# Four early groups of the output projection in the mixer, with the attention's space handed to the FFN's weights

## The chip, the cores and the metric

The kernel runs on one core of a Trainium2 chip. The time is the device time of one execution in microseconds (us); lower is better. TensorE (PE) multiplies, PEld is its loading of weights, VectorE (DVE) and ScalarE (ACT) work elementwise, GpSimd (POOL) does masks and issues the weight DMAs of the staged parts, SyncE (SP) issues the other DMAs. TensorE writes into PSUM, which has 8 banks.

## The reference

Two layers over 528 tokens (16 learned meta tokens ahead of 512) of width 1024, each with a mixer and an FFN:

```python
def mixer_sublayer(h, ...):
    u = rms_norm(h, pre_g)
    z = einsum("bld,de->ble", u, w_in)
    q, k, v, f_logit, a_val, a_gate, sc_b, sc_c, sc_x = split(z)
    y_attn = forgetting_attention(q, k, v, log_sigmoid(f_logit + b_forget))   # 8 heads of 64
    a = a_val * sigmoid(a_gate)
    a = causal_depthwise_conv(a, a_dw_w) + a_dw_b                             # 31 taps, 256 channels
    y_conv = silu(layer_norm(a, a_ln_g, a_ln_b)) @ a_pw_w
    y_sc = sc_b * causal_depthwise_conv(sc_c * sc_x, sc_conv_w)               # 3 taps, 256 channels
    y = concat([y_attn, y_conv, y_sc])
    return h + rms_norm(head_rms_norm(y, head_g) @ w_out, post_g)

def ffn_sublayer(h, ...):
    z = causal_depthwise_conv(rms_norm(h, pre_g) @ w_up, conv_w)              # 3 taps, 2 x 2816 channels
    g, up = split(z, 2)
    return h + rms_norm((silu(g) * up) @ w_down, post_g)
```

All of it is in float32.

## The kernel before

Everything lies transposed: 128 channels on the partitions, tokens along a row, in two halves of 264 (`H`), `hf` 0 and 1. A float32 product is made of three passes over rounded parts, `hi*hi + lo*hi + hi*lo` (`mm3`, line 671), so each block of 128 output channels and each of its 8 blocks `k` of inputs costs three matmuls for a half. A weight block is brought by a DMA into `raw`, ACT casts it to `whi` (L625) and DVE makes the rest `wlo` (L629). `raw` has 3 buffers. `whi` and `wlo` have 3 buffers each in the pool of ring "rot" and 5 each (`WIDE`) in the wide pool, which is there only outside the mixers. `wide_ids` tells which blocks go into the wide pool.

The order of instructions on each engine is fixed when the kernel is built. In the mixers and around them a planner (`Flow`) sets it: generators ("threads") emit TensorE's work and yield what they wait for, other engines' operations are queued with priorities, and the planner goes through estimated times. On the chip each engine runs its list in that order.

The mixer first finishes the convolution's gates, then runs these threads together. `fill` makes the projections from `uhi`, `ulo`, with the convolution's tail and the norms as threads that it starts. `maxima` (L1402, L1426) finds each row's maximum of the attention logits with DVE's help (`mcol`). `exponentials` (L1448) makes the logits again and has ACT take the exponentials `p`. `weighing` (L1494) multiplies them with the values, for a pair of heads at a time. `att_norms` (L1560) and `plain_head_norm` (L1176) make the head norms: a product with the matrix `bd` gives the means of squares in a PSUM bank; ACT, DVE, DVE, ACT and DVE then make the normed parts `yhi` (L1163) and `ylo` (L1164). `y` 0 to 3 are attention's, 4 and 5 the convolution's (after a pointwise product with `pw`), 6 and 7 the gated convolution's (`sccx`, L1088).

PSUM banks are handed out by rings in the mixer: "mm" 0 and 1 for projections and all norms and products of the convolutions, "s1" 3 and 4 for maxima and attention's norms, "st" 5 and 6 for logits, "acc" 2 and 7 for the weighing.

`Early` starts part of the output projection `w_out` inside the mixer: the first pair of its 8 blocks (blocks 0 and 1), for each half of the tokens, as the `y` become ready. Half 0 takes banks 0 and 1 once `maxima` and `fill` are over, half 1 takes 5 and 6 once `exponentials` is over too. `finish` then has the rest: it copies the early results out (`evac`: L1693 to `yp`, L759 squares for the norm), makes the products of blocks 2 to 7 from one pair of banks at a time, and follows with the norm, the residual and the FFN's first products.

Attention's tiles (`q`, `k`, `p`, `vals`, sums) lie in a pool `ap` at the right side, which is closed at the mixer's end; the wide pool `wy` for the FFN then opens in that space.

## Time and profile before

| | |
|---|---|
| median of 3 runs | 1301.84 us (1299.65 to 1301.91) |
| profiled execution, its own time | 1300.12 us |
| its span, first to last instruction | 1298.4 us |
| mean granted clock | 0.995 |
| TensorE busy | 1271.5 us, 98% of the span |
| DVE, ACT, POOL busy | 894.8, 612.8, 110.2 us |

"Busy" is the time in which at least one instruction of the engine runs; matmuls overlap, so their count in a stretch says more than the busy time. A row of the waits names the instruction that waited and the one that released it. In a row of a timeline stand start and duration in us, engine, line, operation, output<-inputs, shape, count, and in brackets how long the engine was idle before and what ended that. A line number is that of the kernel before, unless the text says otherwise.

### The profile page before, as it was taken

What the parts mean: (1) busy time and instruction counts of PE and PEld (TensorE: products, weight loads), DVE (VectorE), ACT (ScalarE), POOL (GpSimd) and SP (SyncE); (2) the same over time, 40 slices, a digit from 0 to 9 for tenths busy, and PEclk for the clock granted to TensorE, in tenths of its full rate; (3) what the DMA queues carried; (4) which work ended last, traced back from release to release, by engine and by line L of the source; (5) the groups of instructions that cost most, each with busy time, mean ns of one, the idle gap of its engine ahead of it and who ended that gap; (6) DMA issues with size and microseconds to landing.
All of it is one profiled execution on the core that took longest, in us unless ns stands there. A gap on an engine that the chain in (4) does not pass through costs nothing. (4 is left out here: it accounts for less than half of the span.)

```text
span 1298.4 us, 24320 instructions
## 1 busy us (share of the span) xinstructions
PE 1271.5 (98%) x9922; PEld 1216.3 (94%) x9922; DVE 894.8 (69%) x1563; ACT 612.8 (47%) x1144; POOL 110.2 (8%) x270
## 2 busy tenths in 40 slices
PE   8999999999999999999999999989999999999997
PEld 7989978999999999999999898889999799989997
DVE  7888896688734775677568886756876256636664
ACT  7255568655433442444562445666543234314443
POOL 1311210100000000000203222100000000000000
PEclk9999999999999999999999999999999999999999
DMA  6133123515644556754542453414032222232321
GB/s 222 50 101 80 45 83 100 182 63 200 223 159 158 202 176 235 237 201 145 214 158 98 118 163 122 129 63 147 22 96 96 97 86 92 72 119 89 92 72 65
DMA packets 55440, 164.57 MB, mean 127 GB/s; under 512 B 6352, under 2 KB 16720, under 8 KB 55328
## 3 DMA queue, kind: packets, MB, share of 16 engines
q1 hardware_dynamic: 41200, 109.56, 25.5%
q0 software_dynamic: 14128, 53.45, 12.8%
q8 instruction: 78, 1.28, 0.4%
q14 instruction: 34, 0.28, 0.1%
HBM read 131.17 MB, written 27.46 MB: 122 GB/s over the span
## 5 line engine op out<-in xcount | busy, mean ns | idle before, releaser
L671 PE MATMUL psum<-uhi,whi 128*128 128x264 f32 (+1 forms) x1936 | 452.2, 287 | 1.0 <-ACT uhi L1865 0.9
L671 PE MATMUL psum<-ulo,whi 128*128 128x264 f32 (+1 forms) x1936 | 445.1, 284 | 0.5 <-DVE ulo L1867 0.4
L671 PE MATMUL psum<-uhi,wlo 128*128 128x264 f32 (+1 forms) x1936 | 444.7, 283 | 0.0
L671 PEld LDWEIGHTS psum<-uhi,whi 128*128 128x128 f32 x1936 | 322.5, 188 | 3.2 <-ACT uhi L1865 1.1
L671 PEld LDWEIGHTS psum<-ulo,whi 128*128 128x128 f32 x1936 | 322.1, 188 | 1.8 <-DVE ulo L902 0.6
L671 PEld LDWEIGHTS psum<-uhi,wlo 128*128 128x128 f32 x1936 | 322.3, 189 | 0.0
L671 PE MATMUL psum<-yhi,whi 128*128 128x264 f32 (+3 forms) x888 | 250.3, 305 | 6.7 <-ACT whi L625 2.2
L671 PE MATMUL psum<-yhi,wlo 128*128 128x264 f32 (+3 forms) x888 | 247.2, 300 | 0.9 <-DVE wlo L629 0.7
L671 PE MATMUL psum<-ylo,whi 128*128 128x264 f32 (+3 forms) x888 | 247.0, 300 | 0.6 <-DVE ylo L1164 0.5
L476 ACT CAST whi<-raw 128x1024 fp32r<-128x1024 f32 (+1 forms) x110 | 113.1, 1030 | 184.6 <-PE psum L671 146.1
L477 DVE TENSOR_TENSOR wlo<-raw,whi 128x1024 fp32r<-128x1024 f32 (+1 forms) x110 | 131.7, 1199 | 65.0 <-ACT whi L476 63.3
L671 PEld LDWEIGHTS psum<-yhi,whi 128*128 128x128 f32 x888 | 160.4, 190 | 14.6 <-ACT yhi L1163 2.6
L671 PEld LDWEIGHTS psum<-ylo,whi 128*128 128x128 f32 x888 | 160.6, 190 | 7.0 <-DVE ylo L1164 1.3
L671 PEld LDWEIGHTS psum<-yhi,wlo 128*128 128x128 f32 x888 | 160.8, 190 | 6.6 <-DVE wlo L629 1.3
L1968 DVE SCALAR_TENSOR_TENSOR c<-z,pv,c 128x528 f32<-128x528 f32 (+1 forms) x176 | 131.9, 756 | 2.7
L617 POOL DMA_DIRECT2D raw<-in_w_dram x60 | 32.1, 535 | 922.2 <-DVE wlo L477 703.9
L629 DVE TENSOR_TENSOR wlo<-raw,whi 128x1024 fp32r<-128x1024 f32 (+2 forms) x64 | 75.7, 1197 | 30.9 <-ACT whi L625 30.5
L987 DVE SCALAR_TENSOR_TENSOR cacc<-apad,pv,cacc 128x528 f32<-128x528 f32 x120 | 87.5, 763 | 0.9
L625 ACT CAST whi<-raw 128x1024 fp32r<-128x1024 f32 (+2 forms) x64 | 64.6, 1028 | 30.7 <-PE psum L671 16.0
L1978 ACT ACTIVATE c<-c 128x528 f32<-128x528 f32 (+1 forms) x44 | 28.1, 639 | 84.0 <-DVE c L1968 84.0
L1986 ACT CAST yhi<-c 128x528 fp32r<-128x528 f32 (+1 forms) x44 | 27.5, 625 | 84.4 <-DVE c L1982 84.2
L1966 ACT ACTIVATE c<-z,pv 128x528 f32<-128x528 f32 (+1 forms) x88 | 63.4, 727 | 0.1
(223 smaller groups left out, 1473.1 us busy)
## 6 DMA issues: line engine op xcount, KB each, us to landing
raw<-in_w_dram SPq DMA_DIRECT2D x116, 512.0 KB
raw<-in_w_dram POOLq DMA_DIRECT2D x44, 512.0 KB, 4.3
split_w<-whi SPq DMA_DIRECT2D x20, 512.0 KB
split_w<-wlo SPq DMA_DIRECT2D x20, 512.0 KB
whi<-split_w POOLq DMA_DIRECT2D x20, 512.0 KB, 4.7
wlo<-split_w POOLq DMA_DIRECT2D x20, 512.0 KB, 6.2
raw<-in_w_dram SPq DMA_DIRECT2D x20, 448.0 KB
raw<-in_w_dram POOLq DMA_DIRECT2D x12, 448.0 KB, 3.6
```

Source lines behind the costliest of these rows:

```text
L476: nc.scalar.copy(hi[:, :sz], raw[:, :sz])
L477: nc.vector.tensor_sub(lo[:, :sz], raw[:, :sz], hi[:, :sz].bitcast(F32))
L617: nc.gpsimd.dma_start(to, src)
L625: nc.scalar.copy(box["hi"][:, :sz], box["raw"][:, :sz])
L629: nc.vector.tensor_sub(lo[:, :sz], box["raw"][:, :sz], box["hi"][:, :sz].bitcast(F32))
L671: nc.tensor.matmul(d, lhsT=w[a][:, k, cols], rhs=rhs(b, k, hf), start=start and i == 0 and p == 0, stop=stop and i == n - 1 and p == 2)
L987: nc.vector.scalar_tensor_tensor(conv[j], in0=src, in1=conv[j], scalar=col("a_dw_w", CK * j + i), op0=ALU.mult, op1=ALU.add)
L1966: nc.scalar.activation(dst, src[:, 2:2 + 2 * fw], AF.Copy, scale=wtap(2, t))
L1968: nc.vector.scalar_tensor_tensor(dst, in0=src[:, i:i + 2 * fw], scalar=wtap(i, t), in1=dst, op0=ALU.mult, op1=ALU.add)
L1978: silu = nc.scalar.activation(cs[0], cs[0], AF.Silu)
L1986: nc.scalar.copy(ghi, cs[0])
```

## The change

- `Early` now works on four groups, named `(m0, hf)`: blocks 0 and 1 and also blocks 2 and 3, for both halves. `(0, 1)` begins when `exponentials` is over, `(0, 0)` when `maxima` and `fill` are. `(2, 0)` begins in banks 2 and 3 when all four attention threads are over, `(2, 1)` in banks 4 and 7 when the mixer is.
- When the attention threads are over, the pool `ap` is closed inside the mixer, the wide pool is opened in its place and the planner is given blocks 2 and 3, which `wide_ids` now puts there (with 6 and 7, instead of 5 to 7). The tile `pw` moves to the pool `mp`, since the convolution still needs it.
- PSUM: "s1" becomes banks 4 and 7, "acc" 2 and 3. The norms and products of the convolutions take a bank of "acc", or else of "mm"; `grab` can wait for the sooner of several rings.
- `finish` copies the four early groups out in a thread of its own and makes products for blocks 4 to 7. The rings of the FFN's start take over the banks of the early groups.

```diff
-            if m > KD - SPLIT[c[0]]:
+            if m > KD - SPLIT[c[0]] + (c[0] == "w_out") or c[0] == "w_out" and m in (2, 3):
                 out.add(i)
...
-    def grab(self, ring, slot=None):
+    def grab(self, ring, slot=None, *more):
         while True:
-            t = ring.slots[0].time
-            ...
-            yield [Head(ring)]
+            for r in (ring, *more):
+                t = r.slots[0].time
+                if t is not None and t <= self.pe:
+                    slot = slot or Slot()
+                    r.take(slot)
+                    return slot
+            yield [Soonest([Head(r) for r in (ring, *more)])]
...
-        ap = ms.enter_context(tc.tile_pool(name=f"ap{l}", bufs=1, side="right", reuse_waits="tile"))
-        banks = {"mm": Ring((0, 1)), "s1": Ring((3, 4)), "st": Ring((5, 6)), "acc": Ring((2, 7))}
+        aps = ExitStack()
+        ap = aps.enter_context(tc.tile_pool(name=f"ap{l}", bufs=1, side="right", reuse_waits="tile"))
+        banks = {"mm": Ring((0, 1)), "s1": Ring((4, 7)), "st": Ring((5, 6)), "acc": Ring((2, 3))}
...
-                ps, slot = yield from bank("mm")
+                ps, slot = yield from bank("acc","mm")
...
-        pw_place[0] = lambda: T(ap, [P, 1024], F32R, "pw")
+        pw_place[0] = lambda: T(mp, [P, 1024], F32R, "pw")
...
-            if over >= {"maxima", "fill"} and 0 not in early.t and name in ("maxima", "fill"):
+            if name == "exponentials":
+                early.begin(0, 1, PAIRS[1], *banks["st"].slots)
+            if over >= {"maxima", "fill"} and name in ("maxima", "fill"):
                 pair = list(banks["mm"].slots)
                 banks["mm"].slots = banks["s1"].slots
-                early.begin(0, PAIRS[0], *pair)
-            if over == {"maxima", "fill", "exponentials"}:
-                early.begin(1, PAIRS[1], *banks["st"].slots)
+                early.begin(0, 0, PAIRS[0], *pair)
+            if over >= attention and name in attention:
+                pair = list(banks["acc"].slots)
+                banks["acc"].slots = banks["s1"].slots
+                aps.close()
+                opened.append(wide_pool(f"wy{l}"))
+                plan_w(after_mixer[l] + 2)
+                early.begin(2, 0, 2, *pair)
...
-        flow.run(lambda: len(over) == 3 and flow.settled())
-        return y, y_at, early
+        flow.run(lambda: len(over) == 5 and flow.settled())
+        early.begin(2, 1, 4, *banks["s1"].slots)
+        return y, y_at, early, opened[0]
...
-        wxs = wide_pool(f"wy{l}", [early.slot[hf] for hf in range(2)])
+        taken = [[early.slot[2, hf], Slot()] for hf in range(2)]
+        for (one, also), i in zip(taken, (3, 7)):
+            also.buf = i
+            also.close(one)
+        p_rings([early.slot[0, hf] for hf in range(2)], *taken)
```

The order of instructions moves as follows at the places of which the prediction speaks. TensorE at the end of layer 0's mixer, from the last head norm's matmul on, before (`whi_249` and `whi_266` are blocks 0 and 1):

```order
L1176 MATMUL psum_1_67<-apad_290_2667,bd_11_93 128x264
L671 MATMUL psum_1_67<-yhi5_292_2678,whi_249_2239 128x264
L671 MATMUL psum_1_67<-ylo5_293_2679,whi_249_2239 128x264
L671 MATMUL psum_1_67<-yhi5_292_2678,wlo_253_2299 128x264
L671 MATMUL psum_1_67<-yhi5_292_2678,whi_266_2430 128x264
L671 MATMUL psum_1_67<-ylo5_293_2679,whi_266_2430 128x264
L671 MATMUL psum_1_67<-yhi5_292_2678,wlo_271_2467 128x264
L671 MATMUL psum_1_67<-yhi4_294_2690,whi_249_2239 128x264
```

and the same place after (`whi_286` and `whi_288` are blocks 2 and 3; lines are those of the changed kernel):

```order
L1181 MATMUL psum_1_67<-apad_290_2686,bd_11_93 128x264
L675 MATMUL psum_1_67<-yhi2_225_2041,whi_288_2661 128x264
L675 MATMUL psum_1_67<-ylo2_226_2042,whi_288_2661 128x264
L675 MATMUL psum_1_67<-yhi2_225_2041,wlo_294_2701 128x264
L675 MATMUL psum_1_67<-yhi3_270_2526,whi_286_2643 128x264
L675 MATMUL psum_1_67<-ylo3_271_2527,whi_286_2643 128x264
L675 MATMUL psum_1_67<-yhi3_270_2526,wlo_289_2672 128x264
L675 MATMUL psum_1_67<-yhi3_270_2526,whi_288_2661 128x264
```

Before, products on `y5` of the first half follow at once, and those on the second half, which wait for this norm, after 12 matmuls. Now products of the new groups with attention's `y` stand there, and 45 matmuls in all before the first that needs this norm. In layer 1 it is 54.

TensorE in layer 1, at the end of the last head's maxima (`mcol`) and the start of its logits (`q30`), before:

```order
L1402 MATMUL psum_1_67<-k30_764_7985,q30_772_7993 128x264
L1448 MATMUL psum_1_67<-q20_770_7991,k20_762_7983 16x16
L1448 MATMUL psum_1_67<-q21_771_7992,k21_763_7984 16x16
L1402 MATMUL psum_1_67<-k30_764_7985,q30_772_7993 128x264
L1426 MATMUL psum_1_67<-ident_r_6_76,mcol_907_9554 1x16
L1426 MATMUL psum_1_67<-ident_r_6_76,mcol_907_9554 1x128 x4
L1448 MATMUL psum_1_67<-q30_772_7993,k30_764_7985 128x16
L1448 MATMUL psum_1_67<-q31_773_7994,k31_765_7986 128x16
```

and after:

```order
L1431 MATMUL psum_1_67<-ident_r_6_76,mcol_906_9559 1x16
L1431 MATMUL psum_1_67<-ident_r_6_76,mcol_906_9559 1x128 x3
L1453 MATMUL psum_1_67<-q20_770_7991,k20_762_7983 16x16
L1453 MATMUL psum_1_67<-q21_771_7992,k21_763_7984 16x16
L675 MATMUL psum_1_67<-uhi_16_106,whi_885_9370 128x264
L675 MATMUL psum_1_67<-ulo_17_107,whi_885_9370 128x264
L675 MATMUL psum_1_67<-uhi_16_106,wlo_886_9371 128x264
L675 MATMUL psum_1_67<-uhi_16_106,whi_885_9370 128x264
L675 MATMUL psum_1_67<-ulo_17_107,whi_885_9370 128x264
L675 MATMUL psum_1_67<-uhi_16_106,wlo_886_9371 128x264
L675 MATMUL psum_1_67<-uhi_16_106,whi_885_9370 128x264
```

Nine matmuls of a projection (`uhi`, `ulo`) now stand between the maxima's rows, the last of which follows them, and six more behind that one. In layer 0's last round nine such matmuls come in as well.

ACT behind the last `y` of layer 0, before and after:

```order
L1163 CAST yhi4_294_2690<-cacc_279_2546 128x264
L1693 ACTIVATE yp_304_2782<-psum_1_67,pg0_3_70 128x264 x2
L759 ACTIVATE acc_313_2813<-psum_1_67 128x528
L1693 ACTIVATE yp_304_2782<-psum_1_67,pg0_3_70 128x264 x2
L759 ACTIVATE acc_314_2828<-psum_1_67 128x528
L625 CAST whi_315_2837<-raw_258_2319 128x1024
L625 CAST whi_316_2849<-raw_312_2797 128x1024
L625 CAST whi_318_2853<-raw_272_2473 128x1024
```

```order
L1168 CAST yhi4_297_2715<-cacc_277_2552 128x264
L1708 ACTIVATE yp_305_2832<-psum_1_67,pg0_3_70 128x264 x2
L763 ACTIVATE acc_314_2861<-psum_1_67 128x528
L1708 ACTIVATE yp_305_2832<-psum_1_67,pg0_3_70 128x264 x2
L763 ACTIVATE acc_317_2887<-psum_1_67 128x528
L1708 ACTIVATE yp_305_2832<-psum_1_67,pg0_3_70 128x264 x2
L763 ACTIVATE c_318_2905<-psum_1_67 128x528
L629 CAST whi_319_2914<-raw_313_2847 128x1024
L629 CAST whi_320_2926<-raw_315_2863 128x1024
L629 CAST whi_323_2941<-raw_316_2881 128x1024
```

Two groups were copied out ahead of the casts of blocks 2, 3 and 4; now three are, ahead of the casts of blocks 4, 5 and 6.

## The prediction

> **What bounds the kernel now.** I read the page first, then TensorE's waits in both layers' mixers, then its matmuls per stretch with the clock, then the timeline of single places.

> ```profile
> span 1298.4 us, 24320 instructions
> PE 1271.5 (98%) x9922; PEld 1216.3 (94%) x9922; DVE 894.8 (69%) x1563; ACT 612.8 (47%) x1144; POOL 110.2 (8%) x270
> ```

> TensorE is busy 1271.5 of 1298.4 us, so only its waits and its slow stretches can be won: 26.9 us in all, start and end of the program among them. The waits of TensorE (what it waits for, total, times, longest) in the late mixers, layer 0 (60 to 200, 200 to 232 us) and then layer 1 (690 to 823, 810 to 875 us):

> ```profile
> PE psum L1448 <- ACT q L1429: 0.8, 1, 0.8
> ...
> PE psum L1426 <- DVE mcol L1409: 0.3, 1, 0.3
> ...
> PE psum L671 <- ACT yhi L1163: 1.5, 1, 1.5
> PE psum L671 <- DVE ylo L1164: 0.5, 2, 0.3
> ...
> PE psum L1448 <- ACT q L1429: 0.9, 1, 0.9
> PE psum L1296 <- DVE gt L1288: 0.5, 1, 0.5
> ...
> PE psum L671 <- DVE sccx L1088: 2.5, 1, 2.5
> PE psum L1426 <- DVE mcol L1409: 0.7, 2, 0.5
> PE psum L671 <- ACT yhi L1163: 0.7, 1, 0.7
> PE psum L671 <- ACT acc L759: 0.5, 1, 0.5
> PE psum L1448 <- ACT q L1429: 0.2, 1, 0.2
> ```

> Layer 0 waits at its mixer's end for the last head norms (yhi, ylo). Layer 1 waits for the gated convolution's DVE operation, for the norms and for the copy that frees an early pair's banks. Both have waits in the last rounds of the attention's maxima (mcol, q). The same places by stretches (TensorE busy, matmuls, granted clock):

> ```profile
> 217.82:221.23 3.41, 1.68 (x11) 1.00 0.00 0
> 221.23:224.65 3.42, 3.42 (x17) 0.50 0.00 0
> 224.65:228.06 3.41, 3.41 (x30) 1.00 0.00 0
> ...
> 821.92:825.33 3.41, 2.35 (x16) 1.00 0.42 154
> 825.33:828.75 3.42, 3.42 (x10) 0.51 0.00 0
> ...
> 842.40:845.81 3.41, 1.57 (x13) 1.00 0.80 244
> ```

> After 217.82:221.23 (11 matmuls) and after 821.92:825.33 (16, half of them tiny) a stretch follows at half clock. "Busy" hides that: 17 matmuls instead of 30 is 13 x 0.114 us (3.41/30) = 1.5 us lost.

> **The change, part by part.** Every engine issues the same instructions, the 9,660 matmuls among them, and SP's queue keeps their order. What changes is what stands where on the other engines.

> *Two more groups begin inside.* Each group is 2 blocks x 8 k x 3 products for one half of the tokens, 48 matmuls. There were two before the last y is needed; now there are three, and a fourth right behind. So 48 more matmuls per layer can stand in front of products on the last y, and 48 more behind them need nothing new. Their price each comes from a full stretch:

> ```profile
> 240.00:250.00 10.00, 10.00 (x84) 10.00 (x84) 3.87 (x4) 4.58 (x8) 1.25 (x3) 1.00 0.54 176
> ```

> 10/84 = 0.119 us, so 5.7 us of cover per layer; this caps what a layer can win here. The end of layer 0, where the norms' last two matmuls and what waits for them stand:

> ```profile
> 216.16 0.61 PE L1176 MATMUL psum<-apad,bd 128*128 128x264 f32 x2
> ...
> 220.28 0.51 PE L671 MATMUL psum<-yhi,whi 128*128 128x264 f32 x2 [1.47 <-ACT yhi L1163]
> ...
> 220.57 0.99 DVE L1164 TENSOR_TENSOR ylo<-cacc,yhi 128x264 fp32r<-128x264 f32 x2
> ```

> From the end of the matmuls (216.77) to the last ylo (221.56) it is 4.8 us. Before, 12 matmuls (1.4 us) stood between; in the order of the changed kernel 45 do (5.4 us), so the wait is covered, by 0.6 us. In layer 1 it is 54 matmuls (6 us). I take layer 0's waits as gone, 1.5 + 0.5 = 2.0, and its half-clock stretch too, 1.5: together 3.5 us. Bounds: 0 if the norms' chain slides as far as the work put ahead of it, 3.5 if not; nearer 3.5, since the matmuls from the norm to the y are what the row prices.

> *Layer 1's end.* The 2.5 us wait: the products of the pointwise convolution need a bank of the ring "mm", and that is held by a result that DVE takes late:

> ```profile
> 844.88 0.76 DVE L1067 SCALAR_TENSOR_TENSOR sccx<-cxp,pv,sccx 128x528 f32<-128x528 f32 x1
> ...
> 845.90 0.42 DVE L1088 TENSOR_TENSOR sccx<-psum,sccx 128x264 f32<-128x264 f32 x1
> ```

> Now these products take a bank of "acc" first, which the last weighing has left, and on DVE L1088 stands 6 rows behind the last weighing's L1527 instead of 17. With the yhi wait (0.7) and the wait for the early copy (0.5, now 48 matmuls away) that is 3.7 us, bounds 1.2 and 3.7; I take 3.7, since the bank that is waited for is no longer asked for.

> *Norms share banks, so projections can run on.* Before, the convolution's norms took their banks from the projections' ring, and in layer 1's last round of maxima no projection stands. Now 15 projection matmuls stand around its mcol and q waits. There: 0.7 + 0.2 of waits and half of a 3.4 us stretch at half clock, 1.7: 2.6 us, of which I take two thirds, 1.7 (the first mcol wait, 0.5, has nothing new right ahead of it). Layer 0's mcol and q, 0.3 + 0.8, get 9 matmuls: half, 0.5. Bounds 0 and 3.7 for both.

> *What the new order may cost.* All rounds of attention are laid out anew, and the trace does not show the new ones. Nearest are the two rows of layer 1's earlier rounds, 0.9 + 0.5: I take as much again as new waits, -1.4, bounds +1.4 (these vanish) and -4.

> *Blocks 2 and 3 come inside, into the attention's space.* The casts are ACT's and DVE's as before (block 2, 3 and 4 were cast right after the mixer) and now stand among the norms' rows. The last reads of what lay there, the weighings', come before the norms whose end opens the pool, so I cost the new wait for that space at nothing. Late next is block 4. The rows behind the last y:

> ```profile
> 221.66 0.85 ACT L1693 ACTIVATE yp<-psum,pg 128x264 f32<-128x264 f32 x2 [0.56 <-DVE ylo L1164]
> 222.40 0.61 ACT L759 ACTIVATE acc<-psum 128x528 f32<-128x528 f32 x1
> 222.89 0.49 ACT L1693 ACTIVATE yp<-psum,pg 128x264 f32<-128x264 f32 x1
> ...
> 224.41 2.94 ACT L625 CAST whi<-raw 128x1024 fp32r<-128x1024 f32 x3
> ...
> 225.49 3.50 DVE L629 TENSOR_TENSOR wlo<-raw,whi 128x1024 fp32r<-128x1024 f32 x3 [3.93 <-ACT whi L625]
> ...
> L629 DVE TENSOR_TENSOR wlo<-raw,whi x14: 1217/1224/1227, 180.5 to 255.5; 128x1024 fp32r<-128x1024 f32 x14
> L625 ACT CAST whi<-raw x13: 1046/1049/1060, 191.8 to 254.0; 128x1024 fp32r<-128x1024 f32 x13
> ...
> DMA to landing us min/median/max: 3.5/4.1/4.8
> ```

> Copying one group takes 222.89 - 221.66 = 1.23 us, and three groups now stand ahead of block 4's cast: 3.8 us after the last y. Its low half is there 225.49 + 1.22 - 224.41 = 2.3 us later, at 6.1. TensorE has 12 + 48 matmuls first, 7.1 us. So block 4 is hidden with 1.0 us to spare (its load, 4.1 us, is issued inside the mixer; if it were issued only with the last y it would land at 4.1, still ahead of the cast's turn or 0.3 behind). Cost 0, at worst 1 us a layer. The copies through banks 4 and 7 have the same shapes: nothing.

> Sum: 3.5 + 3.7 + 1.7 + 0.5 - 1.4 = 8.0 us. The profiled execution took 1300.12, so 1292.1; the median of the runs shown, 1301.84, is 1.7 above it, so **1293.8**.

> [...]

> **Rivals.**
> 1. The half-clock stretches stay, from whatever sets them. [...] Also, 13 matmuls in 842.40:845.81 brought none, 11 and 16 did, so the limit isn't told by busy time. Against: both followed a stretch thinned by waits that are now filled. Without 1.5 and two thirds of 1.7: gain 5.4, 1296.4.
> 2. Only the ends win; the new rounds of attention wait as much more as the old. Without 1.7 and 0.5, and with 3.4 of new waits: 7.2 - 3.4 = 3.8, 1298.0. For it: nothing in these rounds is measured yet.
> 3. It doesn't do what it says: the norms' chain slides behind the added matmuls, the casts of blocks 2 and 3 (1.05 and 1.22 us each) stand in it, and block 4 comes late. Gain 0 to 1.5, about 1301. Against: the counts 45 and 54.
> 4. Slower: norms now take the weighing's banks. One holds a bank this long in layer 1 (its matmul at 850.56):

> ```profile
> 851.21 0.48 ACT L1141 ACTIVATE rs_r<-psum,c_rms 128x264 f32<-128x264 f32 x1 [0.82 <-PE psum L1176]
> ...
> 852.80 0.43 DVE L1146 SCALAR_TENSOR_TENSOR rs_t<-psum,rs_t 128x264 f32<-128x264 f32 x1
> ```

> to 853.23, 2.7 us. There are eight weighings; from 1.0 us of wait in each the gain is gone, and half of the hold, 1.4, gives 11.2 - 8.0 = 3.2 us slower, 1305. Against: before, nothing waits for "acc", and most norms stand far from a weighing.

> **How the numbers follow.** Forecast 0.52, rival 1 0.10, rival 2 0.18, rival 3 0.12, rival 4 0.08. A difference of 0.2% (2.6 us) is about what a measurement of this kernel can tell from none. Faster by more: the forecast, rivals 1 and 2 (2 lies near the edge), 0.80; within: most of 3, 0.11; slower: 4 and a little of 3, 0.09. The lower end, 1288, is both caps (11.4) against the fastest run shown, 1299.65; the upper end, 1300, takes in rivals 1 and 2 and part of 3.

> **What would show it.** Right: no wait for yhi or ylo ahead of the FFN in either layer, 30 matmuls in each 3.41 us there, no half-clock stretch but at start and end, no wait of a pw product for sccx. Wrong: a wait of L671 for whi or wlo behind the mixers (block 4), waits of L1494's first matmul for an rs_t or a norm's ACT row (rival 4), or new waits of L1402, L1426, L1448 beyond 6 us in all.

## The result and the profile after

The changed kernel takes 1284.97 us (median of 4 executions, 1283.5 to 1287.62) against 1301.78 us (1299.65 to 1301.91) before: a ratio of 0.9877, 95% interval 0.9856 to 0.9897. That is 16.8 us less, where 8.0 were forecast. The profiled execution of the changed kernel took 1287.62 us, 2.65 above its median; that of before lay 1.7 below its own. So 12.5 us of the difference can be followed through the two profiles (1298.4 to 1285.9 us).

The page of the changed kernel, span and busy time:

```profile
span 1285.9 us, 24315 instructions
PE 1266.1 (98%) x9922; PEld 1215.7 (95%) x9922; DVE 894.5 (70%) x1563; ACT 610.3 (47%) x1144; POOL 112.5 (9%) x270
```

TensorE's busy time fell too, by 5.4 us, for the same 9,922 matmuls (the page's count; the prediction's text says 9,660). The rows below show one stretch of each layer, with the same work inside: from about the mixer's first matmul on `gt` (L1296), ahead of the first row maxima, to the last matmul with `om_d`, that of the second norm behind the mixer. A row gives its start and end, its length, TensorE's busy time, matmuls, granted clock, the DMAs' share and GB/s. Before:

```profile
73.00:280.00 207.00, 202.29 (x1599) 0.99 0.30 94
712.00:924.00 212.00, 205.43 (x1627) 0.99 0.38 116
```

and after:

```profile
73.76:277.63 203.87, 200.95 (x1599) 0.99 0.31 96
709.75:910.97 201.22, 200.69 (x1627) 1.00 0.39 122
```

Layer 1 gave 10.8 us: its idle time went from 6.6 us (212.00 - 205.43) to 0.5, and its busy time fell by 4.7. Layer 0 gave only 3.1 here. The next rows show what TensorE still waits for in the changed kernel's mixers, from 60 to 200, 200 to 262 and 690 to 810 us; from 810 to 880 us the view has no row at all:

```profile
PE psum L1453 <- ACT q L1434: 1.0, 1, 1.0
PE psum L1301 <- DVE gt L1293: 0.5, 1, 0.5
PE psum L1407 <- DMA k<-sq: 0.5, 1, 0.5
PE psum L1453 <- ACT p L1462: 0.2, 1, 0.2
...
PE psum L812 <- DVE acc L772: 0.9, 1, 0.9
...
PE psum L1301 <- DVE gt L1293: 0.5, 1, 0.5
PE psum L1565 <- DVE sq L1531: 0.2, 1, 0.2
```

The waits for `yhi`, `ylo`, `sccx`, `mcol` and for the early copies are gone. New are 1.0 us for `q` (line 1434 is 1429 of before) in layer 0's second round and 0.9 us for `acc` in the norm behind layer 0's mixer. At the ends of the two mixers, stretches of 3.41 us now hold 28 to 31 matmuls. Before, two in a row held 11 and 17 at layer 0's end, and these two 21 each at layer 1's:

```profile
862.88:866.29 3.41, 2.71 (x21) 1.00 0.00 0
866.29:869.70 3.41, 2.80 (x21) 1.00 0.00 0
```

and after, at layer 0's end and then layer 1's:

```profile
219.41:222.82 3.41, 3.41 (x31) 1.00 0.95 330
222.82:226.23 3.41, 3.41 (x30) 1.00 0.01 2
...
850.00:853.41 3.41, 3.41 (x28) 1.00 1.07 394
853.41:856.82 3.41, 3.41 (x31) 1.00 0.72 243
```

### The profile page after: what moved, and what is told of

The parts are those of the page before. It is cut to its first block, busy times and chain, and to the rows that moved or that the text cites. A ratio compares the mean times of both kernels' runs of the same rounds, so it can differ in the third digit from the quotient of the medians.

```text
span 1285.9 us, 24315 instructions
## 1 busy us (share of the span) xinstructions
PE 1266.1 (98%) x9922; PEld 1215.7 (95%) x9922; DVE 894.5 (70%) x1563; ACT 610.3 (47%) x1144; POOL 112.5 (9%) x270
## 5 line engine op out<-in xcount | busy, mean ns | idle before, releaser
L675 PEld LDWEIGHTS psum<-yhi,whi 128*128 128x128 f32 x888 | 160.1, 190 | 11.4 <-ACT whi L629 2.8
L621 POOL DMA_DIRECT2D raw<-in_w_dram x60 | 32.2, 538 | 918.6 <-DMA raw<-in_w_dram 361.2
L633 DVE TENSOR_TENSOR wlo<-raw,whi 128x1024 fp32r<-128x1024 f32 (+2 forms) x64 | 75.3, 1197 | 15.1 <-ACT whi L629 14.9
L629 ACT CAST whi<-raw 128x1024 fp32r<-128x1024 f32 (+2 forms) x64 | 64.1, 1030 | 14.6 <-PE psum L675 8.3
```

Source lines behind the costliest of these rows:

```text
L621: nc.gpsimd.dma_start(to, src)
L629: nc.scalar.copy(box["hi"][:, :sz], box["raw"][:, :sz])
L633: nc.vector.tensor_sub(lo[:, :sz], box["raw"][:, :sz], box["hi"][:, :sz].bitcast(F32))
L675: nc.tensor.matmul(d, lhsT=w[a][:, k, cols], rhs=rhs(b, k, hf), start=start and i == 0 and p == 0, stop=stop and i == n - 1 and p == 2)
```

## The experiments

Three theories were tested. A: the added groups cover the mixers' ends, and the sharing of banks clears layer 1's last maxima, as forecast, with sizes that were too small. B: the sharing of banks does nearly all of it. C: any new layout of the rounds moves the time by this much. Each time is a median of 4 to 11 executions, beside executions of the kernel before on the same chip (1301.7 to 1302.0 us).

| kernel | us | against before | ratio, 95% interval |
|---|---|---|---|
| before, an unrelated planner estimate changed | 1300.03 | -1.8 | 0.9980 to 0.9998 |
| before, products of `pw` share banks | 1297.95 | -4.0 | 0.9960 to 0.9983 |
| before, norms share banks | 1290.52 | -11.5 | 0.9898 to 0.9925 |
| before, both share banks | 1291.46 | -10.3 | 0.9908 to 0.9935 |
| changed, nothing shared | 1291.06 | -10.7 | 0.9909 to 0.9934 |
| changed, two early groups | 1296.79 | -4.9 | 0.9951 to 0.9976 |
| changed, two groups, banks kept for norms | 1292.96 | -8.9 | 0.9917 to 0.9944 |
| changed, three early groups | 1285.06 | -16.9 | 0.9857 to 0.9884 |
| changed, the planner estimate changed | 1284.36 | -17.5 | 0.9859 to 0.9886 |
| changed, 40 matmuls ahead of the start | 1285.27 | -16.5 | 0.9860 to 0.9887 |
| changed, ACT copies `q` first | 1285.85 | -16.1 | 0.9860 to 0.9890 |
| changed, weight casts yield to the norm | 1296.07 | -5.8 | 0.9939 to 0.9963 |

**The changed kernel without sharing.**

```diff
-                ps, slot = yield from bank("acc","mm")
+                ps, slot = yield from bank("mm")
```

The edit is made at all four places. 

> The changed kernel with one part undone: the norms and products of the convolutions take a bank of "mm" only, as before. Theory A (the groups cover the mixers' ends, and the sharing of banks clears layer 1's last rounds of maxima): the 2.5 us wait for sccx in layer 1 and about 2.6 us of waits and half clock around its last mcol and q come back, so 1290 us, 5 above the changed kernel, and the ends stay free of waits for yhi and ylo. Theory B (the sharing does nearly all of it, since norms that need not wait for a projection's bank end earlier, and the two groups little): 1296 or more. Theory C (any new order of the rounds shifts the waits by this much, no part is needed): between 1282 and 1290 with other waits at other places.

The time is 1291.06, near the 1290 of theory A and far from the 1296 of theory B. TensorE's waits from 690 to 810 and 810 to 880 us (line 1453 is 1448 of before, 1431 is 1426):

```profile
PE psum L1453 <- ACT q L1434: 0.9, 1, 0.9
PE psum L1301 <- DVE gt L1293: 0.5, 1, 0.5
...
PE psum L1431 <- DVE mcol L1414: 0.7, 2, 0.5
PE psum L1453 <- ACT q L1434: 0.2, 1, 0.2
```

These are the waits of the rounds before, to the tenth, and the mixers' ends are clear. But the wait for `sccx` did not return, though its products are back on "mm"; theory A had counted 2.5 of its 5 us on it, so its time came out partly by luck. In the profiles layer 1's stretch takes 205.67 us here and 201.22 in the changed kernel: 2.1 us more idle time and 2.3 more busy time.

**The sharing alone, and its two halves.** Here the kernel before gets the opposite edit: at all four places, at the products of `pw` alone, or at the norms' three places alone.

```diff
-                ps, slot = yield from bank("mm")
+                ps, slot = yield from bank("acc","mm")
```

> The kernel before with the sharing of banks alone (norms and products of the convolutions take a bank of "acc", or else of "mm"; the rings' numbers as before, two groups). Theory A: what sharing gives without groups, 5 us from 1301.8, so 1296 to 1297, with the waits at layer 0's end still there. Theory B: 1290 or less. Theory C: anything from 1293 to 1303.

> The kernel before, where only the pointwise convolution's products may take a bank of "acc"; the norms keep to "mm". If these products' bank is what layer 1's 2.5 us wait for sccx is about, that wait goes and the waits for mcol and q stay: 1298 to 1299.5 us. If what matters is that the norms leave "mm" to the projections, it is within 1 us of 1301.7.

> The kernel before, where only the norms may take a bank of "acc"; the pointwise products keep to "mm". If the two parts add up to the 10.3 us of both (1291.5 us), 1294 to 1295 us. If the norms do nearly all, since "mm" is then free for the products too, 1291 to 1293 us, without the wait for sccx.

Both together gave 10.3 us (1291.46): much more than theory A's 5, and a little short of theory B's 1290. The norms alone gave 11.5 and the products 4.0. So neither theory holds alone: the sharing without the added groups and the groups without the sharing each win over 10 us.

With the norms' sharing alone the two stretches of the layers are 3.4 and 7.8 us shorter than before, 5.1 us of it idle time and 6.1 busy time:

```profile
72.80:276.37 203.57, 199.70 (x1599) 1.00 0.31 96
708.51:912.74 204.23, 201.95 (x1627) 1.00 0.39 120
```

The waits of that kernel from 200 to 262 and from 690 to 880 us (its line numbers are one above those of before):

```profile
PE psum L672 <- ACT yhi L1164: 1.3, 1, 1.3
PE psum L672 <- ACT acc L760: 0.5, 1, 0.5
PE psum L672 <- DVE ylo L1165: 0.3, 1, 0.3
...
PE psum L1297 <- DVE gt L1289: 0.5, 1, 0.5
PE psum L1561 <- DVE sq L1527: 0.2, 1, 0.2
...
PE psum L672 <- ACT yhi L1164: 0.8, 1, 0.8
PE psum L672 <- ACT acc L760: 0.5, 1, 0.5
PE psum L672 <- DVE ylo L1165: 0.3, 1, 0.3
```

The rounds of layer 1 are clear of `q`, `mcol` and `sccx`; the ends wait about as before. With the products alone it is the other way round: `sccx` gone, `q` 0.9, `mcol` 0.7 and `q` 0.2 still there. The profile with the norms' sharing also has no half-clock stretch inside the two layers, where the one of before has two; these are at most 3.4 of the 6.1 us of busy time. Whether the gain comes from the projections, which keep "mm", or from the norms, which get a bank sooner, was not separated. The projection that `sccx` waits for is taken 10 us earlier (835.62 instead of 845.90 us), which speaks for the projections.

**Two groups, and three.** The first run is the changed kernel without the groups `(2, 0)` and `(2, 1)`, the second the same with banks 2 and 3 left to the norms, the third the changed kernel with `(2, 0)` and without `(2, 1)`. Below stand the lines that go in the first run, and then those that go besides in the second:

```diff
-                early.begin(2, 0, 2, *pair)
...
-        early.begin(2, 1, 4, *banks["s1"].slots)
```

```diff
-                pair = list(banks["acc"].slots)
-                banks["acc"].slots = banks["s1"].slots
                 aps.close()
```

> The changed kernel with only the first two groups begun inside; the sharing of banks, the closing of the attention's space and the early casts of blocks 2 and 3 stay. Theory A: the waits for yhi and ylo at both mixers' ends come back, 2.0 us and a half-clock stretch of 1.5 us in layer 0, 0.7 + 0.5 us in layer 1, so 1289 to 1290 us. Theory B: 1285 to 1287, since the norms are early enough. Theory C: no return of these waits in particular.

> The kernel with two early groups of the run before (1296.8 us), but banks 2 and 3, which it takes from the convolution's norms when attention is over and leaves idle, stay with the norms; the early casts of blocks 2 and 3 remain. In the order of TensorE the last norms then stand where they stand in the kernel before with sharing alone (1291.5 us), 39 matmuls earlier. If giving away the two banks is what made two groups 5.3 us slower than sharing alone, this one takes 1291 to 1292 us. If the casts of blocks 2 and 3 among the norms' rows did it, 1295 to 1297.

> The changed kernel without the fourth group: blocks 2 and 3 of the second half are made after the mixer, as in the kernel before. The last norms keep their place and the third group stands behind them. If the third group's 48 matmuls are what covers the norms, it takes 1285 us within 1.5, with no wait for yhi or ylo. If the fourth group covers what comes next (the copies of the groups, block 4's casts: ready by estimate 6.1 us after the last y, against 1.4 us of matmuls without it), it waits 3 to 5 us more in each layer: 1291 to 1295 us.

Without the groups the waits for `yhi` return, in layer 0 (200 to 262 us) and layer 1 (810 to 880 us), and the time is 1296.79, worse than any theory said:

```profile
PE psum L675 <- ACT yhi L1168: 1.5, 1, 1.5
PE psum L675 <- DVE ylo L1169: 0.7, 2, 0.4
PE psum L1181 <- DVE rs_t L1151: 0.6, 1, 0.6
...
PE psum L675 <- ACT yhi L1168: 2.3, 1, 2.3
```

About half of the excess was the experiment's own doing: it still took banks 2 and 3 from the norms and left them idle. With these banks kept the time is 1292.96; so giving them away costs 3.8 us when nothing uses them. That is above the 1291 to 1292 expected for this case and below the 1295 to 1297 of the other; the 1.5 us above sharing alone are within the two intervals. The ends of this run wait longer than before the change, 2.3 + 0.4 us in layer 0 and 2.3 + 0.3 in layer 1, and the changed kernel is 8.0 us faster than it: that is what the added groups are worth once the banks are shared. With three groups the time is 1285.06, without a row for `yhi`: the third group is enough for the ends. The estimate of 3 to 5 us for the other case was ill founded: in the order, the products of `(2, 1)` stand at the same place, behind the third group, whether begun early or made by `products()`, so this run takes no cover away from block 4. It shows that beginning the fourth early is worth nothing that can be measured.

**Another layout.** `HOP = 0.08` for `0.06` in both kernels.

> The kernel before with one planner estimate changed that is no part of the change: 0.08 instead of 0.06 us from one engine to the next. Every round is laid out slightly otherwise. Theory C (the layout of the rounds by itself moves the time by as much as the change's parts do): 3 us or more away from 1301.7, either way. Theories A and B (the parts act by what they release): within 2 us of 1301.7.

> The changed kernel with the same planner estimate of 0.08 us. Theory C: 3 us or more away from 1285, and nearer to the kernel before with the same estimate than 16.8 us would say. Theories A and B: within 2 us of 1285, and the distance to the kernel before with this estimate stays 14 to 19 us.

The kernel before moved by 1.8 us, the changed kernel by 0.6, and the distance is 15.7 us. By this one other layout, theory C is out as the cause: a new layout alone moved the time by 2 us at most.

**The start and the clock.** `WARM` is 40 instead of 20, and the order of TensorE behind it is the same.

> The changed kernel with 40 instead of 20 matmuls on a constant tile at the start, ahead of the first weight, which TensorE waits for until 8.1 us; the order behind them is the same. If a half-clock stretch follows a stretch thinned by waits, and which waits thin one depends on where the stretches fall in a run, then the two half-clock stretches of the profiled start (8.1 to 14.9 us) go, the median falls by 1 to 2 us to about 1283.5, and the times lie closer together than the 4.1 us between 1283.5 and 1287.6. If the start's half clock has another cause, the time is the same within 1 us and the stretches stay; if the added matmuls delay the first weight's, it is up to 1 us slower.

The median stayed at 1285.27, against the 1283.5 expected if the start's stretches were what costs, and the four times still spread over 2.9 us (1283.47 to 1286.35). The profiled execution, the fastest of the four, has no half-clock stretch but the last one (its mean granted clock is 1.000, the changed kernel's 0.996), so it shows the changed order undisturbed. It also allows a useful comparison. Below are the stretch with the wait for `q` at 124 us and the one behind it, in the changed kernel and then here:

```profile
124.12:127.54 3.42, 2.24 (x13) 1.00 0.35 79
127.54:130.95 3.41, 3.38 (x16) 0.50 0.47 153
...
123.37:126.78 3.41, 2.43 (x13) 1.00 0.35 79
126.78:130.20 3.42, 3.42 (x30) 1.00 0.45 159
```

Both stretches hold 13 matmuls and the same wait of 0.95 us, cut a little otherwise by the 3.41 us stretches: once half clock follows, once not.

**ACT's place for `q`.** At L1434 of the changed kernel `prio=-1` stands for `prio=0`.

> The changed kernel, where ACT's copy of a row's maxima into q (L1434) has rank over the casts of k. At layer 0's round at 124 us, where TensorE waits 0.95 us for that copy (and half a clock followed in the profile: 124.12 to 127.54, then 3.41 us at half), one cast of 0.38 us no longer stands ahead. If the copy's place is what that wait is for, it falls to about 0.57 and the half-clock stretch behind it is rarer: 1283.5 to 1284.5 us, the time lowest yet. If the new order of the later rounds costs as much, 1285 and above.

The wait for `q` fell to 0.6 us, but the next, for `p` (0.2), became 0.7: the same sum, and no gain (1285.85). The mean granted clock of that profiled execution is 0.995, against 0.996 in the changed kernel's, so half clock did not become rarer in it.

**The norm behind layer 0's mixer.** From its first matmul with `om_d` to the last of the second norm, start to start, it lasts 32.2 us in the changed kernel's profile and 29.8 before. ACT there:

```profile
246.49 0.48 ACT L822 ACTIVATE rs<-psum,c_rms 128x264 f32<-128x264 f32 x1 [0.92 <-PE psum L812]
248.09 1.05 ACT L629 CAST whi<-raw 128x1024 fp32r<-128x1024 f32 x1 [1.12 <-DMA raw<-in_w_dram]
249.04 0.42 ACT L825 ACTIVATE rs<-rs 128x264 f32<-128x264 f32 x1
```

The norm's second row, L825, stands behind a cast whose weight is late: 2.1 us after the first row's end. In the profile with 40 matmuls at the start the order is the same, the weight is there, and L825 begins at 245.29 for a first row at 243.98; the whole lasts 30.9 us there. The experiment let the casts give way:

```diff
-WP = 0
+WP = 1
...
-YE = YF = 9; YM = 4
+YE = 9; YF = 0.9; YM = 4
```

> The changed kernel, where in the output projection's end the cast of an FFN weight block gives way to a row of the norm that is about to be ready (the planner's priority of these casts 1 instead of 0, and it may leave ACT idle for a row of higher rank). On ACT in layer 0 the norm's three rows L822, L825, L826 then follow each other, with no cast that waits for a weight's DMA between them (in the changed kernel's profile L825 stands 2.1 us behind L822 for such a cast). If that cast is why layer 0's stretch from the norm to the FFN's fourth product lasts 32.2 us instead of 29.8, it returns to about 30 and the time is 1283, 2 us less. If the late weight itself sets that stretch, the wait only moves to the FFN's products and the time stays at 1285.

It is 11 us slower than the changed kernel. The norm's three rows do follow each other now (246.43, 246.95 and 247.40 us), but the stretch lasts 37.3 us. The mixers' waits are those of the changed kernel, and the new waits stand behind them, in layer 0 (240 to 290 us) and layer 1 (880 to 920 us):

```profile
PE psum L675 <- DVE z L1966: 1.4, 1, 1.4
PE psum L675 <- DVE ulo L906: 0.9, 1, 0.9
PE psum L675 <- ACT uhi L904: 0.7, 1, 0.7
...
PE psum L812 <- DVE acc L772: 3.7, 2, 1.9
```

The edit moved all casts of both layers' ends, not the one, and what was to be freed waits more: neither expectation came true. That the late weight is chance, more than order, is what the two profiles of one order suggest; it is not shown.

## Why the prediction was wrong, and where it was right

The direction was right, and so were the ends of the mixers; what the banks are worth was not, and the time lies below the range. Its lower end, 1288, took twice the 5.7 us of cover (11.4) as all that can be won. That caps what the added groups hide, not what the sharing of banks wins. By its terms:

- **Layer 0's end, 3.5 us: right.** No wait for `yhi` or `ylo`, 31 and 30 matmuls in stretches that held 11 and 17, and they return without the added groups (1.5 + 0.7 us), as the count of 45 matmuls said. The changed kernel without sharing has layer 0's stretch in 203.46 us, 3.5 less than before.
- **Layer 1's end, 3.7 us: right in size, with a reason that holds in part.** The 2.5 us wait for `sccx` goes in three ways, which the times of DVE's row L1088 (845.90 and 852.30 us before) tell apart. With the products alone on "acc" the row still comes late, at 845.39, but the products take another bank and run from 842.73 us on without a wait for it: this is the reason that the prediction gave. With the norms alone on "acc" the row comes early, at 835.62 and 837.47, so the bank is free when the products ask. With the groups and no sharing it is late again, at 844.44, and the products stand still from 838.95 to 844.93, but 44 matmuls of the early groups fill that time. In the changed kernel the row is early, at 836.83 and 838.71, as the prediction's other sign, 6 rows of DVE instead of 17, had it.
- **Norms' banks, 1.7 + 0.5 us, and new waits, -1.4 us: the step that failed.** I looked only at the last round of maxima, and set "as much again as new waits" against it. The norms' sharing by itself is worth 11.5 us (the forecast for all that hangs on banks, with the 2.5 of `sccx`, was 1.7 + 0.5 + 2.5 - 1.4 = 3.3). The wait for `q` in layer 1's earlier round (0.9), which I used as a measure of new trouble, was itself one of the waits that the sharing removes: it is there in the changed kernel without sharing and with the products of `pw` alone shared, and gone in each profile where the norms share. In the mixers there are new waits of 0.2 us in layer 1 and 1.0 + 0.2 in layer 0, where 0.8 + 0.5 + 0.3 + 0.3 + 0.2 went.
- **Busy time: a term that was too small.** The prediction said that only 26.9 us of idle time could be won, slow stretches included, but these lie inside the 1271.5 us of busy time. Of layer 1's 10.8 us, 4.7 are not idle time in any row, where the forecast had two thirds of 1.7. One half-clock stretch of 3.4 us, at most 1.7 us lost, is part of it. The rest shows as matmuls of the same shapes that take less time. In the groups of layer 1 (690 to 880 us or so), before and after, busy and mean ns:

```profile
L1448 PE MATMUL psum<-q,k 128*128 128x16 f32 (+5 forms) x96 | 20.0, 308 | 1.3 <-ACT q L1429 1.1
L1402 PE MATMUL psum<-k,q 128*128 128x264 f32 (+4 forms) x48 | 12.7, 302 | 0.0
L1607 PE MATMUL psum<-apad,om_c 128*128 128x264 f32 x8 | 3.0, 516 | 0.0
...
L1453 PE MATMUL psum<-q,k 128*128 128x16 f32 (+5 forms) x96 | 18.2, 292 | 0.0
L1407 PE MATMUL psum<-k,q 128*128 128x264 f32 (+4 forms) x48 | 12.2, 295 | 0.0
L1612 PE MATMUL psum<-apad,om_c 128*128 128x264 f32 x8 | 2.2, 402 | 0.0
```

  Logits, maxima and the layer norm's means take 3.1 us less in these three rows, apart from the 1.3 us of idle time that the first shows. Some of it lies in the half-clock stretch, and one row goes the other way (`yhi,pw`, 3.3 to 4.0 us). Counted in the two traces from the start of one matmul to the start of the next, against the usual distance for its shape, the 4.7 us are 1.7 in the half-clock stretch, 2.4 right ahead of the idle times that rows show, and some 0.7 elsewhere. A matmul of 128x264 is drawn 0.28 us long, though in a full stretch the next starts 0.12 us behind it (at 15.23, 15.35 and 15.47 us in the changed kernel's profile): so a wait begins under the drawn end of the matmul before, and its row shows too little. By this count most of the rest belongs to the waits that went.
- **Block 4 and the copies, 0 us: right.** No row waits for `whi` or `wlo` behind the mixers. How much cover it needs was not tested, since the run with three groups keeps those matmuls in place.
- **The last step, 1.7 us from profile to median.** I carried before's distance over. The changed kernel's profile lies 2.65 us on the other side, so 4.3 us of the 16.8 come from which executions were profiled. In it stand two half-clock stretches at the start (8.1 to 14.9 us, one before) and one at 127, and the late weight; the profile with 40 matmuls has none of these, and layer 0 takes 201.07 us in it instead of 203.87:

```profile
72.84:273.91 201.07, 199.34 (x1599) 1.00 0.31 97
```

  So layer 0 gives 3.1 to 5.9 us, where the terms above (3.5 + 0.5 - half of 1.4) said 3.3; layer 1 gives 10.8, where they said 4.7.

Of the rivals, 1 (the half-clock stretches stay) is half true: those of the mixers follow thin stretches, but behind the thin stretch at 124 us, in one order of instructions, one profile has half clock and one has not. The wait of 1.5 us for `yhi` that the prediction shows ahead of such a stretch is not the longest of the kernel before: at the start TensorE waits 2.2 us until 8.27 and runs at half clock from 9.58 to 12.99. The changed kernel without sharing has the waits of before's last maxima, and no half clock behind them, where the kernel before has it (its 821.92:825.33, with one matmul and 0.21 us of busy time less than the first row here, and the stretch after):

```profile
818.24:821.65 3.41, 2.56 (x17) 1.00 0.00 0
821.65:825.07 3.42, 3.21 (x19) 1.00 0.00 0
```

Rival 2 (new rounds wait as much) fell with the profile. Rival 4's price, weighings that wait for a norm's bank, does not show in any wait row. A slide of the norms, as in rival 3, is real but where it was measured it has another cause than the casts: the two banks that are taken from them, 3.8 us when no group uses them.

The parts overlap: norms' sharing 11.5, groups without sharing 10.7, both 16.8. The wait for `sccx` is in both sums, and the mixers' ends are worth more once the banks are shared: 8.0 us for the added groups, where the rows of before had 3.5 + 0.7 + 0.5.

## What to carry to other kernels

Give short operations that others wait for (here norms of one or two matmuls) banks that the long filler does not use: here that took all waits for `q` and `mcol` out of layer 1's rounds, not only those that the prediction had priced. Before a stalled end, put work that needs nothing new, as much as the chain is long and no more. When pricing a looser resource, ask which of the waits now in the rows it also removes, before setting them down as the noise of a new layout.

## What the runs showed of the hardware

```profile
857.09:860.51 3.42, 1.08 (x8) 1.00 0.58 194
860.51:863.92 3.41, 3.41 (x16) 0.50 0.00 0
```

Single executions of one kernel differ along with the clock: the kernel before with products of `pw` shared took 1295.92 us at a mean clock of 0.997 and 1301.97 at 0.991.
